# Low parts on VectorE, passes ordered by the weights' part, and a router with stationary weights

## The chip, the cores and the metric

The kernel runs on one core of a Trainium2 chip. The time is device microseconds of one execution; what counts is the median of several. The profile is that of one further execution on the same core.

## The reference

Two layers over 256 tokens of width 1024, with fp32 inputs and weights. Each layer is a token mixer (an mLSTM, a forgetting attention and an RWKV7 branch behind one wide projection), a cross attention to 256 memory tokens and a feed-forward part, each followed by a residual and a layer norm. The first layer's feed-forward part is dense; the second's is a mixture of eight experts of width 3584, of which each token takes two:

```python
def _post_norm(x, sub, g, b):
    return _layer_norm(DEEPNORM_ALPHA * x + sub, g, b)

def _swiglu(x, wgu, wd):
    gate, up = jnp.split(x @ wgu, 2, axis=-1)
    return (jax.nn.silu(gate) * up) @ wd

def _moe(x, router_w, router_b, ex_wgu, ex_wd):
    logits = (x @ router_w).astype(jnp.float32) + router_b
    top_v, top_i = lax.top_k(logits, TOP_K)
    top_w = jax.nn.softmax(top_v, axis=-1)
    comb = jnp.sum(jax.nn.one_hot(top_i, N_EXPERTS) * top_w[..., None], axis=-2)
    y = jnp.zeros_like(x)
    for e in range(N_EXPERTS):
        y = y + comb[..., e:e + 1] * _swiglu(x, ex_wgu[e], ex_wd[e])
    return y

for l in range(DEPTH):
    x = _post_norm(x, _token_mixer(x, ...), *ln1[l])
    x = _post_norm(x, _cross_attention(x, mem_n, *xattn[l]), *ln2[l])
    x = _post_norm(x, _swiglu(x, ...) if l % 2 == 0 else _moe(x, ...), *ln3[l])
```

## The kernel before

**Products in three passes.** Every operand of a large product is held as a high part, its fp32 value rounded to TensorE's fp32r type, and a low part, the difference. `mm3` (L323) adds three products in one PSUM tile: high weights with high x, high weights with low x, low weights with high x. It loops over the blocks `k` of 128 of the contraction and makes the three passes inside.

**Weights.** They pass through the core once, in chunks of 128 x 1024 fp32 (512 KB). `chunk` (L286) starts the load on SyncE's queue into a raw buffer (`raw`, L294), lets ScalarE cast it into the high part (`whi`, L295) and lets VectorE or GpSimd subtract for the low part (`wlo`, L297). GpSimd takes a low part when the list `self.aside` says so. `out_proj` (L389) fills that list, with `ASIDE = 3` entries that are true, at each of the five projections that end in a residual and a layer norm through it (the mixer's and the cross attention's in both layers, the dense part's in the first): 15 chunks of 912 in all. `out_proj` loads its last chunks, calls `mid()` and loads the norm's scale and shift before it issues its last products; this is so before and after.

**Buffers.** Rings of buffers are taken least recently used first: three raw buffers and three pairs of parts at the start, four more of each from the cross attention on, six more raw ones in the experts.

**Layer norm.** `residual` (L378) adds the projection's PSUM tile to x in two halves of 512 columns; `moments` (L351) takes statistics on VectorE and the power -0.5 on GpSimd (L364); `layer_norm` applies them on VectorE (L373, L374) half by half; `to_fm` (L339) transposes each half on TensorE and splits it into `xh` on ScalarE (L335) and `xl` on VectorE (L336). The two token halves are `tt`, the two column halves `h`.

**Experts' part.** `moe` (L1148) makes the logits of each token half with 16 products (L1195): a 128 x 128 block of x's high or low part is loaded as the stationary operand, and the router's 16 columns (high and low part of eight experts, `rwp`) move. VectorE adds bias and both parts (L1198, L1199), finds the two best (L1200, L1201), makes one-hot rows and counts (L1202 to L1211) with small products against triangular and all-one matrices (L1208 to L1213). ScalarE and GpSimd split x, tokens on partitions, into `xth` and `xtl` (L1220, L1221). `order` ranks the experts by their number of tokens. `experts` (L1283) gathers the tokens of a pair of experts by products with a 0/1 matrix `epb` (L1300, L1315); a pair has a large expert (128 slots, `mm3`) and a small one (64 slots). There are four pairs; `expert` runs over seven steps `c` of 512 hidden columns: `block` (L1343) the projections, `down` (L1365) the way back. In the small expert's `block` (L1355) the high and low parts of its x stand side by side as one stationary operand, and each block of weights moves twice, high and low part.

**Order.** The tile framework orders the instructions of each engine from a simulated timeline and from the order in which the program emits them, and puts in the semaphores; each engine then executes its list in order.

## Time and profile before

| | |
|---|---|
| median of 3 executions | 2165.76 us (2164.92 to 2166.17) |
| the profiled execution | 2165.97 us |
| its span, first to last instruction | 2164.2 us |
| mean granted clock of TensorE | 0.987 |
| TensorE, VectorE, ScalarE, GpSimd busy | 96%, 74%, 56%, 11% of the span |
| moved by the transfers | 532.18 MB, 246 GB/s on average |

A line of the profile gives busy time of an engine or of a group of instructions. Products on TensorE are pipelined, so the busy time of one is longer than the step from its start to the next. The rows below are in microseconds from the start of the span, if nothing else is said; a duration with xN is that of N such operations in a row.

### The profile page before, as it was taken

The page shows a single profiled execution, that of the slowest core. Times are in us where ns is not written, and L with a number is a line of the kernel's source. Part 1 is how long each engine was busy: PE and PEld are TensorE (multiplying, and loading weights), DVE is VectorE, ACT ScalarE, POOL GpSimd, SP SyncE. Part 2 cuts the span into 40 slices and gives each one's busy share as a digit, 9 for nine tenths or more (in the row PEclk, how much of TensorE's full clock was granted, in tenths as well). Part 3 has the DMA queues.
Part 4 walks back from the last instruction along what each step waited for, and adds up shares of the span by engine and source line. Part 5 has one row for each costly group of instructions (what it writes and reads, how often), then busy time and mean ns, then how long its engine had stood idle before and what let it go on. Part 6 is the DMA issues. An engine that isn't in the chain of part 4 may idle for free.

```text
span 2164.2 us, 33290 instructions
## 1 busy us (share of the span) xinstructions
PE 2082.1 (96%) x11726; PEld 1724.1 (80%) x11726; DVE 1601.9 (74%) x2327; ACT 1222.3 (56%) x1723; POOL 227.6 (11%) x332
## 2 busy tenths in 40 slices
PE   7999999999999899999998899999999999999996
PEld 6988898989998788889887777777767767777674
DVE  6776656746555677665675698889888988899887
ACT  5443334544443544332453587777777777777774
POOL 0031142202001113114212100000000000000000
PEclk9999999999999999999999799999999999999998
DMA  5431335645553543133574599999999999999994
GB/s 199 157 120 59 135 123 200 253 151 202 189 185 124 173 152 111 62 104 111 214 263 146 179 366 393 389 363 363 388 388 363 372 386 385 391 354 372 379 393 181
DMA packets 146767, 532.18 MB, mean 246 GB/s; under 512 B 16672, under 2 KB 17184, under 8 KB 145568
## 3 DMA queue, kind: packets, MB, share of 16 engines
q1 hardware_dynamic: 142128, 520.16, 64.9%
q10 hardware_dynamic: 4080, 8.77, 1.2%
q8 instruction: 94, 1.54, 0.3%
q0 software_dynamic: 384, 1.05, 0.1%
q14 instruction: 81, 0.66, 0.1%
HBM read 525.19 MB, written 4.72 MB: 245 GB/s over the span
## 4 chain that ended last, share of the span: by engine, by line
PE 52%; DMA 12%; DVE 10%; issue 3%; ACT 2%; POOL 1%; SPq 0%; DVEq 0%; ACTq 0%; POOLq 0%
DVE wlo L297 8%; DMA raw<-in_ex_wgu 7%; PE fps L331 7%; PE ops L331 6%; PE dps L331 6%; PE xps L331 5%; DMA raw<-in_ex_wd 5%; PE eacc L1372 4%; PE egu L331 4%; PE egu L1355 4%; PE eacc L331 2%; PE eacc L1379 2%; PE ups L331 2%; ACT whi L295 2%; PE eg L1315 1%
## 5 line engine op out<-in xcount | busy, mean ns | idle before, releaser
L297 DVE TENSOR_TENSOR wlo<-raw,whi 128x1024 fp32r<-128x1024 f32 x897 | 1073.9, 1231 | 261.4 <-ACT whi L295 251.5
L295 ACT CAST whi<-raw 128x1024 fp32r<-128x1024 f32 x912 | 916.2, 1049 | 468.0 <-PE fps L331 159.8
L331 PE MATMUL fps<-xh,whi 128*128 128x256 f32 x816 | 238.6, 293 | 7.5 <-ACT cu L543 4.9
L331 PE MATMUL fps<-xl,whi 128*128 128x256 f32 x816 | 235.0, 288 | 3.2 <-DVE xl L336 3.2
L331 PE MATMUL fps<-xh,wlo 128*128 128x256 f32 x816 | 236.4, 290 | 0.2
L1355 PE MATMUL egu<-wlo,xgs 128*128 128x512 f32 x448 | 198.1, 443 | 12.2 <-DVE wlo L297 12.2
L331 PE MATMUL egu<-wlo,xgh 128*128 128x512 f32 x448 | 178.9, 401 | 2.7 <-DVE wlo L297 2.6
L331 PE MATMUL egu<-whi,xgh 128*128 128x512 f32 x448 | 179.1, 401 | 0.8 <-ACT esl L1390 0.8
L331 PE MATMUL egu<-whi,xgl 128*128 128x512 f32 x448 | 178.2, 398 | 0.0
L1355 PE MATMUL egu<-whi,xgs 128*128 128x512 f32 x448 | 178.0, 398 | 0.0
L331 PEld LDWEIGHTS fps<-xh,whi 128*128 128x128 f32 x816 | 156.1, 191 | 13.9 <-ACT cu L543 5.7
L331 PEld LDWEIGHTS fps<-xl,whi 128*128 128x128 f32 x816 | 156.0, 191 | 5.7 <-DVE xl L336 3.5
L331 PEld LDWEIGHTS fps<-xh,wlo 128*128 128x128 f32 x816 | 156.0, 191 | 3.0 <-issue 2.0
L364 POOL TENSOR_TENSOR lnve<-lnve,mhalf 128x1 f32<-128x1 f32 x14 | 14.5, 1038 | 1282.2 <-DVE lnve L363 1282.2
L1355 PEld LDWEIGHTS egu<-wlo,xgs 128*128 128x128 f32 x448 | 84.0, 188 | 74.8 <-DVE wlo L297 60.9
L331 PE MATMUL eacc<-whi,ehl 128*128 128x512 f32 x448 | 124.6, 395 | 0.0
L331 PEld LDWEIGHTS egu<-wlo,xgh 128*128 128x128 f32 x448 | 84.7, 189 | 26.9 <-DVE wlo L297 7.8
L1372 PE MATMUL eacc<-raw,ehf 128*128 128x512 f32 x224 | 104.8, 594 | 0.1
L331 PEld LDWEIGHTS egu<-whi,xgl 128*128 128x128 f32 x448 | 84.8, 189 | 20.2 <-issue 0.7
L331 PEld LDWEIGHTS egu<-whi,xgh 128*128 128x128 f32 x448 | 84.5, 189 | 20.0 <-ACT esl L1390 1.0
L331 PEld LDWEIGHTS eacc<-whi,ehl 128*128 128x128 f32 x448 | 83.8, 188 | 20.0 <-DVE ehl L336 0.2
L331 PE MATMUL dps<-xl,whi 128*128 128x256 f32 x352 | 98.9, 281 | 0.6 <-DVE xl L336 0.6
(427 smaller groups left out, 4048.2 us busy)
## 6 DMA issues: line engine op xcount, KB each, us to landing
raw<-in_ex_wgu SPq DMA_DIRECT2D x448, 512.0 KB, 6.0
raw<-in_ex_wd SPq DMA_DIRECT2D x224, 512.0 KB, 5.8
raw<-in_w_fm SPq DMA_DIRECT2D x54, 512.0 KB, 3.3
raw<-in_w_gate SPq DMA_DIRECT2D x48, 512.0 KB, 3.2
raw<-in_ff_wgu SPq DMA_DIRECT2D x44, 512.0 KB, 4.3
raw<-in_w_tm SPq DMA_DIRECT2D x24, 512.0 KB, 3.3
raw<-in_ff_wd SPq DMA_DIRECT2D x22, 512.0 KB, 4.3
raw<-in_w_out SPq DMA_DIRECT2D x16, 512.0 KB, 3.9
```

Of the source, the lines that this page charges most:

```text
L295: nc.scalar.copy(hi[:, :e], raw[:, :e])
L297: eng.tensor_tensor(lo[:, :e], raw[:, :e], hi[:, :e].bitcast(F32), op=OP.subtract)
L331: nc.tensor.matmul(ps, l, r, start=first and n == 0, stop=last and n == 3 * kt - 1)
L364: nc.gpsimd.tensor_tensor(ve[:, 1:2], ve[:, 0:1], self.mhalf[:, 0:1], op=OP.pow)
L1315: nc.tensor.matmul(ps[:, kk, :n * P], src[:, tt, o], pb[:, tt, lo:hi].rearrange("p a b -> p (a b)"), start=tt == 0, stop=tt == 1)
L1355: nc.tensor.matmul(ps, x[2][:, 2 * q + kk], part[:, kk], start=q + kk + n == 0, stop=q == 3 and kk == 1 and n == 1)
L1372: nc.tensor.matmul(acc[h], ht[0][:, i], w[:, h * 512:(h + 1) * 512], start=f, stop=l)
L1379: nc.tensor.matmul(acc[h], ht[1][:, i - 2].rearrange("p a b -> p (a b)"), part[:, 0, s], start=f and n == 0, stop=l and n == 1)
```

## The change

Three edits.

1. All low parts go to VectorE: the list `aside` is gone, and the four subtractions for `xtl` move from GpSimd to VectorE, in a loop of their own behind ScalarE's four casts.
2. The pass is the outer loop in `mm3`: high weights with high x for every block `k`, then high weights with low x, then low weights with high x. In the small experts' `block`, both blocks take the high weights first, then both the low ones.
3. In the router the weights are stationary (128 x 16) and x moves (128 columns). The logits come out with the 16 columns on partitions; ScalarE copies them to SBUF, and a small product with a 16 x 8 matrix `fold`, made on GpSimd, brings the tokens back on partitions and adds high and low part. One addition of the bias is left. Conversion, one-hot rows, their sum and the positions are made for both token halves at once.

```diff
--- before.py
+++ after.py
@@ -58,7 +58,6 @@
 
 
 AHEAD = 2000
-ASIDE = 3
 FIRST = 65536.0
 RAWS = 6
 XGS = 5
@@ -293,8 +292,7 @@
         lo = pool.tile([P, 1024], F32R, name="wlo", tag="wlo", bufs=nparts)
         nc.sync.dma_start(raw[:, :e], src)
         nc.scalar.copy(hi[:, :e], raw[:, :e])
-        eng = nc.gpsimd if self.aside and self.aside.pop(0) else nc.vector
-        eng.tensor_tensor(lo[:, :e], raw[:, :e], hi[:, :e].bitcast(F32), op=OP.subtract)
+        nc.vector.tensor_tensor(lo[:, :e], raw[:, :e], hi[:, :e].bitcast(F32), op=OP.subtract)
         f = lambda t: t[:, :e].rearrange("p (k n) -> p k n", k=kt)
         return f(hi), f(lo)
 
@@ -324,8 +322,8 @@
 
         nc = self.nc
         n = 0
-        for k in range(kt):
-            for a, b in ((wh, xh), (wh, xl), (wl, xh)):
+        for a, b in ((wh, xh), (wh, xl), (wl, xh)):
+            for k in range(kt):
                 w, x = a[:, k, wsl], b[:, k, xsl]
                 l, r = (w, x) if w_stat else (x, w)
                 nc.tensor.matmul(ps, l, r, start=first and n == 0, stop=last and n == 3 * kt - 1)
@@ -402,7 +400,6 @@
         if mid:
             mid()
         gb = self.load_ln(lname)
-        self.aside = [False] * (7 - tail) + [True] * ASIDE
         for tt in range(2):
             for h in range(2):
                 for i, w in enumerate(ws):
@@ -1187,28 +1184,33 @@
             oh = wk.tile([P, 2, 2, NE], F32, name="eoh")
             sel = wk.tile([P, 2, NE], F32, name="esel")
             pos = wk.tile([P, 2, NE], F32, name="epos")
+            fold = wk.tile([2 * NE, NE], F32, name="efd")
+            nc.gpsimd.tensor_tensor(fold, self.ident[:2 * NE, :NE], self.ident[:2 * NE, NE:2 * NE], op=OP.add)
             pp = tp.tile([P, 5, NE], F32, name="epp", tag="t")
             for tt in range(2):
-                lp = self.gp.tile([P, 2, NE], F32, name="elp", tag="g")
+
+                lt = self.gp.tile([2 * NE, P], F32, name="elt", tag="g")
                 for k in range(KD):
                     for part in (xh, xl):
-                        nc.tensor.matmul(lp.rearrange("p a b -> p (a b)"), part[:, k, tt * P:(tt + 1) * P],
-                                         rwp[:, k].rearrange("p a b -> p (a b)"), start=k == 0 and part is xh,
-                                         stop=k == KD - 1 and part is xl)
-                nc.vector.tensor_tensor(lg[:, tt], lp[:, 0], rb, op=OP.add)
-                nc.vector.tensor_tensor(lg[:, tt], lg[:, tt], lp[:, 1], op=OP.add)
+                        nc.tensor.matmul(lt, rwp[:, k].rearrange("p a b -> p (a b)"), part[:, k, tt * P:(tt + 1) * P],
+                                         start=k == 0 and part is xh, stop=k == KD - 1 and part is xl)
+                ls = wk.tile([2 * NE, P], F32, name="els", bufs=2)
+                nc.scalar.copy(ls, lt)
+                nc.tensor.matmul(pp[:, 3 + tt], ls, fold, start=True, stop=True)
+                nc.vector.tensor_tensor(lg[:, tt], pp[:, 3 + tt], rb, op=OP.add)
                 nc.vector.max(mx[:, tt], lg[:, tt])
                 nc.vector.max_index(ix[:, tt], mx[:, tt], lg[:, tt])
-                nc.vector.tensor_copy(ixf[:, tt], ix[:, tt])
-                for k in range(2):
-                    nc.vector.tensor_scalar(oh[:, tt, k], it[:, :NE], ixf[:, tt, k:k + 1], None, op0=OP.is_equal)
-                nc.vector.tensor_tensor(sel[:, tt], oh[:, tt, 0], oh[:, tt, 1], op=OP.add)
+            nc.vector.tensor_copy(ixf, ix)
+            for k in range(2):
+                nc.vector.tensor_tensor(oh[:, :, k], it[:, None, :NE].to_broadcast([P, 2, NE]),
+                                        ixf[:, :, k:k + 1].to_broadcast([P, 2, NE]), op=OP.is_equal)
+            nc.vector.tensor_tensor(sel, oh[:, :, 0], oh[:, :, 1], op=OP.add)
             for tt in range(2):
                 if tt:
                     nc.tensor.matmul(pp[:, 1], ones, sel[:, 0], start=True, stop=False)
                 nc.tensor.matmul(pp[:, tt], self.c('strict'), sel[:, tt], start=tt == 0, stop=True)
-                nc.vector.scalar_tensor_tensor(pos[:, tt], pp[:, tt], 1.0, sel[:, tt], op0=OP.add, op1=OP.mult)
-                nc.vector.tensor_scalar(pos[:, tt], pos[:, tt], -1.0, None, op0=OP.add)
+            nc.vector.scalar_tensor_tensor(pos, pp[:, 0:2], 1.0, sel, op0=OP.add, op1=OP.mult)
+            nc.vector.tensor_scalar(pos, pos, -1.0, None, op0=OP.add)
             for tt in range(2):
                 nc.tensor.matmul(pp[:, 2], ones, sel[:, tt], start=tt == 0, stop=tt == 1)
 
@@ -1218,7 +1220,10 @@
                 for tt in range(2):
                     o = (slice(None), tt, slice(h * 512, (h + 1) * 512))
                     nc.scalar.copy(th[o], xt[o])
-                    nc.gpsimd.tensor_tensor(tl[o], xt[o], th[o].bitcast(F32), op=OP.subtract)
+            for h in range(2):
+                for tt in range(2):
+                    o = (slice(None), tt, slice(h * 512, (h + 1) * 512))
+                    nc.vector.tensor_tensor(tl[o], xt[o], th[o].bitcast(F32), op=OP.subtract)
 
             def order():
 
@@ -1350,8 +1355,8 @@
                         self.mm3(ps, wh, wl, x[0][:, k], x[1][:, k], 2, False, slice(0, 512), slice(0, P),
                                  first=q == 0, last=q == 3)
                         continue
-                    for kk in range(2):
-                        for n, part in enumerate((wh, wl)):
+                    for n, part in enumerate((wh, wl)):
+                        for kk in range(2):
                             nc.tensor.matmul(ps, x[2][:, 2 * q + kk], part[:, kk], start=q + kk + n == 0,
                                              stop=q == 3 and kk == 1 and n == 1)
                 if not small(j):
@@ -1473,7 +1478,7 @@
             for tt in range(2):
                 for h in range(2):
                     self.to_fm(self.tp, xt[:, tt], xh, xl, tt, h)
-        self.rings, self.aside, self.used, self.count = [], [], {}, 0
+        self.rings, self.used, self.count = [], {}, 0
         self.stream(self.ctx, 3, 3)
         stop = self.dbg.get('stop', 99)
         for l in range(2):
```

## Rows read from the trace of the kernel before

**Rows 1.** Busy time by stage: stretch, length, engines, TensorE's clock, transfers' share, GB/s.

```profile
0.00:1180.00 1180.00, 1144.24 (x7812) 1028.69 (x7812) 742.32 (x1406) 510.70 (x822) 213.21 (x317) 0.99 0.44 155
1180.00:1220.00 40.00, 27.59 (x121) 25.03 (x122) 28.47 (x73) 12.61 (x23) 12.46 (x14) 0.62 0.39 147
...
1317.00:2131.00 814.00, 796.36 (x3305) 584.10 (x3304) 723.92 (x733) 611.95 (x771) 0.00 (x0) 1.00 0.99 378
```

**Rows 2.** Groups of instructions: busy us, mean ns of one; idle time before.

```profile
L297 DVE TENSOR_TENSOR wlo<-raw,whi 128x1024 fp32r<-128x1024 f32 x897 | 1073.9, 1231 | 261.4 <-ACT whi L295 251.5
...
L297 POOL TENSOR_TENSOR wlo<-raw,whi 128x1024 fp32r<-128x1024 f32 x15 | 42.5, 2857 | 101.6 <-ACT whi L295 101.5
...
L336 DVE TENSOR_TENSOR xl<-tp,xh 128x512 fp32r<-128x512 f32 x24 | 15.8, 679 | 4.2 <-ACT xh L335 4.1
```

**Rows 3.** VectorE's timeline at two layer norms: start, us, operation, count.

```profile
385.31 1.40 DVE L373 SCALAR_TENSOR_TENSOR xt<-lnr,lnmv,lngb 128x512 f32<-128x512 f32 x2
...
390.28 2.83 DVE L297 TENSOR_TENSOR wlo<-raw,whi 128x1024 fp32r<-128x1024 f32 x1
...
500.06 4.74 DVE L373 SCALAR_TENSOR_TENSOR xt<-lnr,lnmv,lngb 128x512 f32<-128x512 f32 x2
```

**Rows 4.** The chain that ended last, by engine (page).

```profile
PE 52%; DMA 12%; DVE 10%; issue 3%; ACT 2%; POOL 1%; SPq 0%; DVEq 0%; ACTq 0%; POOLq 0%
```

**Rows 5.** TensorE's timeline at the start; in brackets the idle time before.

```profile
14.65 0.58 PE L331 MATMUL fps<-xl,whi 128*128 128x256 f32 x1 [3.23 <-DVE xl L336]
15.03 0.41 PE L331 MATMUL fps<-xh,wlo 128*128 128x256 f32 x1
...
18.87 0.32 PE L331 MATMUL fps<-xh,wlo 128*128 128x256 f32 x1
```

**Rows 6.** TensorE's timeline from the last norm to the first gather.

```profile
1186.47 1.94 PE L343 MATMUL tp<-ident,xt 128*128 128x128 f32 x8 [6.93 <-DVE xt L374]
...
1194.64 0.36 PE L1195 MATMUL elp<-rwp,xl 128*128 128x16 f32 x1
...
1197.62 0.36 PE L1195 MATMUL elp<-rwp,xl 128*128 128x16 f32 x1
...
1205.86 0.87 PE L1315 MATMUL eg<-epb,xth 128*128 128x128 f32 x3
```

**Rows 7.** GpSimd's timeline in the same stretch.

```profile
1179.83 2.35 POOL L297 TENSOR_TENSOR wlo<-raw,whi 128x1024 fp32r<-128x1024 f32 x1
...
1183.91 1.63 POOL L364 TENSOR_TENSOR lnve<-lnve,mhalf 128x1 f32<-128x1 f32 x1
...
1198.56 5.04 POOL L1221 TENSOR_TENSOR xtl<-xt,xth 128x512 fp32r<-128x512 f32 x4 [6.89 <-ACT xth L1220]
```

**Rows 8.** VectorE's timeline in the same stretch.

```profile
1180.84 2.55 DVE L373 SCALAR_TENSOR_TENSOR xt<-lnr,lnmv,lngb 128x512 f32<-128x512 f32 x2
...
1198.65 1.21 DVE L1211 TENSOR_SCALAR epos<-epos 128x8 f32<-128x8 f32 x1
...
1202.45 1.32 DVE L1204 TENSOR_SCALAR eoh<-eit,eixf 128x8 f32<-128x8 f32 x2
...
1205.08 0.17 DVE L1211 TENSOR_SCALAR epos<-epos 128x8 f32<-128x8 f32 x1
```

**Rows 9.** Groups of weight loads, of 64 and of 128 columns.

```profile
L331 PEld LDWEIGHTS fps<-xh,whi 128*128 128x128 f32 x816 | 156.1, 191 | 13.9 <-ACT cu L543 5.7
...
L746 PEld LDWEIGHTS fot<-fptb,fv 128*64 128x64 f32 x32 | 3.1, 134 | 2.1 <-issue 0.7
```

**Rows 10.** Waits: who waits, for whom: us, times, longest.

```profile
PEld egu L1355 <- DVE wlo L297: 60.9, 140, 1.1
...
PE egu L1355 <- DVE wlo L297: 12.2, 23, 0.8
```

**Rows 11.** Busy time by stage, ten microseconds each.

```profile
1200.00:1210.00 10.00, 6.16 (x25) 5.70 (x25) 8.22 (x33) 1.32 (x4) 3.60 (x3) 0.50 0.00 0
1210.00:1220.00 10.00, 10.00 (x46) 8.35 (x46) 4.88 (x4) 5.84 (x9) 0.00 (x0) 0.82 0.31 109
```

## Prediction

> **What bounds the kernel now.** I read the busy time by stage first [rows 1]. Up to 1180 us TensorE is the limit: busy 1144 of 1180 us, with VectorE at 742. From 1317 to 2131 us, the steady part of the experts, the transfers have a share of 0.99, TensorE is busy 796 of 814 and VectorE 724: three resources near their end at once. Between them lie 40 us, 1180 to 1220, in which no engine is full: TensorE 27.6 us, transfers 0.39. That is the last layer norm, the router, the counting of slots and the first gather, and it is the one stretch where a chain of short operations sets the time.
>
> The groups of instructions [rows 2] say what the edits can touch. VectorE makes 897 low parts at 1.231 us, GpSimd 15 at 2.857 us; these 15 sit in threes at five of the layer norms. The timeline of VectorE at two of those norms [rows 3] shows their side effect: two halves of a norm take 1.40 us when GpSimd is quiet, and 4.74 us at 500.06; a low part takes 2.83 us beside one of GpSimd's, not 1.23.
>
> The chain that ended last puts 52% on TensorE, 12% on transfers and 10% on VectorE [rows 4], so in the experts' loop nothing that saves one resource saves its full price.
>
> **Start of the kernel: -1.5 us (-2.9 to 0).** After one product with the high part of x TensorE waits 3.23 us, until 14.65, for x's low part [rows 5]. Products of 256 columns then start 0.213 us apart: 19 of them from 15.03 to 18.87, 3.84 / 18, which is TensorE's lower clock level, 1.2 GHz. With the passes outermost, the seven other high products of the first chunk stand ahead of the first that needs the low part: 7 x 0.213 = 1.5 us of work fits into the wait. At most the wait itself goes, less some 0.3 us for handing over: 2.9. Nothing, if the other high parts of x aren't there in time.
>
> **Twelve low parts at the first four norms: -0.4 us (-1 to +1).** VectorE gets 12 x 1.231 = 14.8 us. It gets back the blocking: I estimate four low parts stretched by 1.6 us as at 390.28 (6.4), and 2 us of stretched norm at each of four norms, between the 0 of 385.31 and the 3.3 of 500.06 (8.0) [rows 3]: 14.4 us. So its load there is unchanged. What hides the rest is TensorE, which has products of other chunks to do and is busy 97% of this stage [rows 1]; the norm of each half comes a little earlier. If that cover were gone, all 14.8 us would be bare; that is the last rival.
>
> **The last norm: -1.4 us (-2.6 to +1.1).** Here there is no cover: TensorE waits 6.93 us for the normalised x, until 1186.47 [rows 6]. The wait is made by GpSimd: its low part of 1179.83 takes 2.35 us, copies follow, and the power for the standard deviation starts at 1183.91 [rows 7], though VectorE had its input done before the norm's first two halves at 1180.84; these took 2.55 us, not 1.40 [rows 8]. Without the low part ahead of it, the power can come some 2.6 us earlier. But that low part, 1.23 us, is now queued on VectorE near by: 2.6 - 1.2 = 1.4. All three of this norm in front of it would make 3.7 - 2.6 = +1.1.
>
> **Router with narrow weights: -1.5 us (-2.7 to +0.7).** Now x is loaded (128 columns) and 16 columns move; the rows from 1194.64 to 1197.62 are 15 products, so one each 2.98 / 14 = 0.213 us, 32 in all [rows 6]. After the change 16 columns are loaded and 128 move. No row has such a shape. It can't be worse than 0.213: the gather's products from 1205.86 load 128 columns and move 128 at that step (0.87 us for three with the drain of the last). Below, half of a 256-column product at this clock gives 0.107 [rows 5]. I take 0.12, nearer to the moving columns, since 64-column loads are shorter too, 134 ns against 191 ns for 128 columns [rows 9]. Of 32 x 0.093 = 3.0 us, the products between two waits for x's parts give nothing back. The 15 from 1194.64 on stand behind the last low part and count in full; of the 17 others I count 8, those that hold up transposes of the other token half: 23 x 0.093 = 2.1. Against it stand a copy of 128 columns on ScalarE (0.25, an estimate between the 0.17 of VectorE's smallest operations [rows 8] and the 0.68 of its 512 columns [rows 2]), a small product that folds high and low (0.6, an estimate: a step of 0.213 and the handovers on both sides), less one addition on VectorE (0.2): +0.65. Together -1.5; the ends are -3.4 + 0.65 and 0 + 0.65.
>
> The Trainium skill, "TensorE: Matmul & The Clock Gate", section LDWEIGHTS (loading the stationary operand), has the load go by columns, one per 1/1.2 ns: 16 columns 13 ns against 107 for 128. The rows agree that fewer columns load faster, not on the size [rows 9]. By that page the load would vanish behind the moving columns, 23 products at 0.107: 2.4 us saved instead of 2.1.
>
> **Counting and gather: -2.7 us (-4.1 to -1.3).** From 1198.56 GpSimd makes the four low parts for the gather, 5.04 us [rows 7]. In the same time five small operations on VectorE, on 2 to 8 columns, take 4.91 us, from the 1.21 at 1198.65 to the two in 1.32 at 1202.45; the first one's line takes 0.17 at 1205.08, after GpSimd is done [rows 8]. At 0.17 each they are 0.85: 4.06 us of blocking on the path from the logits to the first gather at 1205.86. It goes; in its place VectorE itself makes the four low parts, at 0.679 each as x's low parts of the same shape [rows 2], 2.7 us. They stand behind ScalarE's casts and can slip into the gaps in which VectorE waits for the small products; I let half of them fall on the path: -4.06 + 1.35. Merged operations for both token halves save another few tenths, and the first half's positions now wait for the second's; I set these against each other.
>
> **Pass order in the experts: -3.3 us (-6.7 to 0).** In the small experts' projections TensorE's loads wait for a low part 140 times, 60.9 us, and its products 23 times, 12.2 us [rows 10]. With both high parts first, one 512-column product moves ahead of each wait, 0.24 us (796 / 3305 [rows 1]). But the next chunk is as late as before, so per step of the loop I count one product, at most: 28 steps (four pairs of experts, seven each) x 0.24 = 6.7 us. If the transfers pace the loop, at a share of 0.99, it is 0. Half is taken, as the chain gives TensorE the larger part of it [rows 4].
>
> **Sum.** -1.5 - 0.4 - 1.4 - 1.5 - 2.7 - 3.3 = -10.8 us against the profiled execution's 2165.97 (span 2164.2 and 1.8 outside it), which is within 0.01% of the median 2165.76. That gives **2155.2 us**.
>
> **Rivals.**
> *The edges close again (0.20).* The router's edits get nothing: the low parts moved to VectorE stand ahead of the norm (0 for the last norm), the narrow products are no faster than their fold costs (0), half the counting's gain is lost (-1.3), and the loop is paced by transfers, so that pass order does nothing there (0). With -1.5 and -0.4 for the first stage: 2165.97 - 3.2 = 2162.8. For it speaks the 0.99 [rows 1]; against it that VectorE's stretched operations are plainly on the path [rows 8].
> *The clock comes back sooner (0.20).* TensorE runs at 0.50 of its clock from 1200 to 1210 and at 0.82 on average from 1210 to 1220 [rows 11], so the lower level, 1.2 GHz, lasts for 3.6 us of the latter, to 1213.6. Before it rose, TensorE had been busy 6.2 of 10 us and then without a break. The products from 1205.86 [rows 6] to 1213.6 are 7.7 us at that level; if the shorter chain leaves fewer holes and the clock is up by then, half goes, 3.9. With the loop's full 6.7: -10.8 - 3.9 - 3.4 = -18.1, 2147.9.
> *VectorE becomes the limit (0.10, the other side).* 15 x 1.231 + 4 x 0.679 = 21.2 us more on VectorE; if it lands on the path at the norms while the relief falls where nobody waits, and the start (1.5), the narrow router (1.5) and the loop (3.3) still give theirs: +21.2 - 6.3 = +14.9, 2180.9. It decides from 10.6 of the 21.2 bare (6.3 + 4.3). Against it: 742 busy of 1180 [rows 1], and the stretched rows. The Trainium skill, "Perfetto Trace Analysis", section Optimizing Scalar/DVE Operations, speaks for it: with a saturated VectorE, moving work to GpSimd may make sense, which this undoes; the same paragraph doubts it, as the two share a port. The stretched rows are that doubt, measured [rows 3].
>
> **How the numbers follow.** The sum has 0.50, with a range of its own of 2150 to 2160. The range, 2147 to 2163, takes in the two faster-side rivals and leaves out the slower one. A measurement of this kernel tells some 0.2%, 4.3 us, from no change. Faster by more: 0.50 + 0.20 and a quarter of the first rival, 0.75; within it 0.15; slower 0.10.
>
> **What would show it.** No low part on GpSimd, and none of VectorE's at 2.8 us; the halves of all norms at 0.7. TensorE's first wait for x's low part at 1.7 us, not 3.2. The wait before the last transposes at 5.5 us. Router products 0.12 us apart, the small operations of counting at 0.17, the first gather 5 to 6 us sooner; the stretch between the last norm and 1317 shorter by about 6 us, and the steady loop by 3. Wrong would be the prediction if VectorE's low parts push the norms later, if the loop's length moves by more than 7 us either way, since nothing here prices that, or if the order of work elsewhere changes with the new costs.

## The result, and the profile after

The changed kernel takes 2155.01 us (median of 5, 2149.88 to 2155.67) against 2166.17 of before: a ratio of 0.9941, 95% interval 0.9925 to 0.9957. Measured a second time it was 0.9943 (0.9929 to 0.9956). The forecast was 2155.2, in a range of 2147 to 2163. The profiled execution took 2149.88 us, span 2147.7: 16.5 us less span than before's 2164.2. It is the fastest of its five; the median execution is 5.1 us slower. Where the 16.5 us went, stage by stage, is a matter of the trace; that the sum came out is not yet a proof of its terms.

Busy time by stage of the changed kernel, against [rows 1]:

```profile
0.00:1180.00 1180.00, 1144.98 (x7812) 1030.47 (x7812) 742.39 (x1419) 517.55 (x822) 182.58 (x308) 0.99 0.45 155
1180.00:1220.00 40.00, 28.78 (x154) 25.30 (x154) 28.07 (x74) 16.76 (x31) 2.96 (x4) 0.74 0.47 168
...
1317.00:2131.00 814.00, 799.33 (x3336) 591.06 (x3336) 729.32 (x741) 614.74 (x777) 0.00 (x0) 1.00 0.97 376
```

The first 1180 us are as full as they were, 1145 us of TensorE. In the 40 us behind them GpSimd has gone from 12.5 to 3.0 us, the transfers have more, and TensorE's clock is at 0.74, not 0.62. Groups and waits of the changed kernel, against [rows 2, 10]:

```profile
L295 DVE TENSOR_TENSOR wlo<-raw,whi 128x1024 fp32r<-128x1024 f32 x912 | 1088.9, 1230 | 229.3 <-ACT whi L294 196.2
```

```profile
PEld egu L1360 <- DVE wlo L295: 51.9, 113, 1.0
...
PE egu L1360 <- DVE wlo L295: 12.0, 23, 0.5
```

All 912 low parts are VectorE's, at 1.230 us on average. The waits of the small experts' loads are 51.9 us, 113 times; they were 60.9, 140 times.

TensorE's and VectorE's timelines from the last norm to the first gather, against [rows 6, 8], and GpSimd's, against [rows 7]:

```profile
1186.04 1.94 PE L341 MATMUL tp<-ident,xt 128*128 128x128 f32 x8 [6.78 <-DVE xt L372]
...
1191.98 0.31 PE L1195 MATMUL elt<-xh,rwp 128*16 128x128 f32 x1
...
1193.05 0.31 PE L1195 MATMUL elt<-xh,rwp 128*16 128x128 f32 x1
...
1194.29 0.22 PE L1195 MATMUL elt<-xl,rwp 128*16 128x128 f32 x1
1195.32 0.38 PE L1199 MATMUL epp<-efd,els 16*128 16x8 f32 x2 [0.81 <-ACT els L1198]
...
1201.23 1.09 PE L1320 MATMUL eg<-epb,xth 128*128 128x128 f32 x4
```

```profile
1180.63 1.21 DVE L295 TENSOR_TENSOR wlo<-raw,whi 128x1024 fp32r<-128x1024 f32 x1
1181.75 0.20 DVE L359 BATCH_NORM_AGGREGATE lnmv<-lnst 128x2 f32<-128x12 f32 x1
1181.87 1.17 DVE L295 TENSOR_TENSOR wlo<-raw,whi 128x1024 fp32r<-128x1024 f32 x1
...
1183.69 0.15 DVE L361 TENSOR_SCALAR lnve<-lnmv 128x1 f32<-128x1 f32 x1
1183.75 1.41 DVE L371 SCALAR_TENSOR_TENSOR xt<-lnr,lnmv,lngb 128x512 f32<-128x512 f32 x2
...
1195.75 0.16 DVE L1200 TENSOR_TENSOR elg<-epp,rb 128x8 f32<-128x8 f32 x1
1195.83 0.69 DVE L1226 TENSOR_TENSOR xtl<-xt,xth 128x512 fp32r<-128x512 f32 x1
...
1196.51 0.68 DVE L1226 TENSOR_TENSOR xtl<-xt,xth 128x512 fp32r<-128x512 f32 x1
...
1197.30 0.69 DVE L1226 TENSOR_TENSOR xtl<-xt,xth 128x512 fp32r<-128x512 f32 x1
...
1198.11 0.26 DVE L1205 TENSOR_TENSOR eoh<-eit,eixf 128x16 f32<-128x16 f32 x2
...
1200.34 0.17 DVE L1213 TENSOR_SCALAR epos<-epos 128x16 f32<-128x16 f32 x1
```

```profile
1183.92 0.99 POOL L362 TENSOR_TENSOR lnve<-lnve,mhalf 128x1 f32<-128x1 f32 x1 [24.58 <-DVE lnve L361]
```

In before, the first bias addition of the second token half, which ends the router there, is this row:

```profile
1198.02 0.17 DVE L1198 TENSOR_TENSOR elg<-elp,rb 128x8 f32<-128x8 f32 x1 [1.77 <-PE elp L1195]
```

Cut at the same places, the two profiles give this. "The gather" is its run of products, from 1205.86 and from 1201.23; in before a single product of it stands ahead of that run, at 1201.41.

| stretch | before | after | difference |
|---|---|---|---|
| start to TensorE's stop at the last norm (1186.47 - 6.93; 1186.04 - 6.78) | 1179.54 | 1179.26 | -0.3 |
| wait for the norm | 6.93 | 6.78 | -0.15 |
| transposes and router, to the last router product | 11.15 | 8.25 | -2.9 |
| from there to the gather | 8.24 | 6.94 | -1.3 |
| from there to the end of the span | 958.3 | 946.5 | -11.9 |

The norm gave nothing, router and counting together 4.2 us, which is what the two terms said (1.5 + 2.7). The copy and the fold belong to the router's term: cut behind them, at the bias addition (1198.02 before, 1195.75 after), the router gave 1.8 us and the counting 2.4. The experts gave three to four times their term.

Why the norm gave nothing is in VectorE's rows. The power now starts on GpSimd without a stretched neighbour, but at 1183.92; it was 1183.91. On VectorE one low part, 1180.63, stands ahead of the norm's aggregate, and another, 1181.87, between the aggregate and the small operation at 1183.69 from which GpSimd takes its input; the first halves start at 1183.75 in place of 1180.84. What GpSimd held up, VectorE's own queue now holds up.

In the router x's products are 0.107 us apart (11 from 1191.98 to 1193.05, 1.07 / 10). The copy and the fold between the last one and the first addition of the second half take 1.46 us (1194.29 to 1195.75). From there the small operations take 0.17 us each, and the two one-hot rows 0.26. But three of the four low parts of x for the gather stand among them (1195.83, 1196.51, 1197.30), 0.6 us each from its start to the next: 1.8 us on the path, where the prediction let half of the four, 1.35, fall on it.

TensorE's clock after, against [rows 11]:

```profile
1190.00:1200.00 10.00, 6.26 (x47) 5.72 (x45) 6.48 (x27) 3.96 (x9) 0.95 (x2) 0.67 0.30 119
1200.00:1210.00 10.00, 9.73 (x41) 8.67 (x41) 5.37 (x23) 3.75 (x7) 0.00 (x0) 0.65 0.00 1
1210.00:1220.00 10.00, 10.00 (x57) 8.49 (x55) 6.22 (x6) 7.24 (x11) 0.00 (x0) 1.00 0.77 246
```

It is up again for part of the router (0.67), falls once more, and is at its upper level throughout 1210 to 1220. With 0.65 from 1200 to 1210 the lower level ends at 1207.0 (10 x 0.35 / 0.5), 5.8 us after the gather's start; before it was 7.7 us after it.

The start, against [rows 5], and TensorE's waits in the first 62 us (total, times, longest):

```profile
10.74 2.07 PE L329 MATMUL fps<-xh,whi 128*128 128x256 f32 x8 [0.35 <-ACT xh L333]
12.62 2.05 PE L329 MATMUL fps<-xl,whi 128*128 128x256 f32 x8
14.46 1.72 PE L329 MATMUL fps<-xh,wlo 128*128 128x256 f32 x8
```

```profile
PE tp L638 <- DVE grow L635: 2.0, 1, 2.0
PE rza L759 <- ACT lw L762: 1.2, 1, 1.2
...
PE fps L329 <- DVE mv L554: 0.4, 1, 0.4
```

Eight high products run, and the low part of x is there when they end: the wait of 3.23 us is gone. Two waits of 2.0 and 1.2 us further on are new. Only a part of this is the order of passes. Ahead of x's low part VectorE makes two small casts, and these differ between the two profiles, first before, then after:

```profile
11.48 2.52 DVE L270 CAST keep<-cst 128x128 uint8<-128x128 f32 x2
```

```profile
11.38 0.56 DVE L269 CAST keep<-cst 128x128 uint8<-128x128 f32 x2
```

Beside them GpSimd fills a buffer in eight operations, in both kernels. In before the casts end at 14.00 with the last of these (13.86); in the changed kernel they pass between them, and two of the eight take 0.66 us in place of 0.52. Which of the two happens is a matter of the single execution: of the 14 traces of this document, seven have the casts long and seven short, and the three traces that share the changed kernel's first part have both.

### The profile page after: what moved, and what is told of

Read it like the earlier page. It is cut to its first block, busy times and chain, and to the rows that moved or that the text cites. A ratio compares the mean times of both kernels' runs of the same rounds, so it can differ in the third digit from the quotient of the medians.

```text
span 2147.7 us, 33270 instructions
## 1 busy us (share of the span) xinstructions
PE 2071.4 (96%) x11730; PEld 1723.0 (80%) x11730; DVE 1598.2 (74%) x2338; ACT 1227.1 (57%) x1725; POOL 187.4 (9%) x314
## 4 chain that ended last, share of the span: by engine, by line
PE 67%; DMA 11%; DVE 10%; issue 4%; ACT 4%; POOL 3%; SPq 0%; POOLq 0%; DVEq 0%; ACTq 0%
PE fps L329 14%; DVE wlo L295 7%; PE ops L329 7%; DMA raw<-in_ex_wgu 6%; PE xps L329 6%; PE egu L329 6%; PE dps L329 6%; DMA raw<-in_ex_wd 4%; PE egu L1360 4%; PE eacc L1377 4%; PE ups L329 3%; ACT whi L294 3%; PE eacc L329 2%; PE rg L857 2%; PE eacc L1384 1%
## 5 line engine op out<-in xcount | busy, mean ns | idle before, releaser
L329 PE MATMUL egu<-whi,xgh 128*128 128x512 f32 x448 | 142.3, 399 | 0.8 <-ACT esl L1395 0.8
L1360 PE MATMUL egu<-whi,xgs 128*128 128x512 f32 x448 | 141.1, 397 | 0.7 <-ACT whi L294 0.7
L329 PE MATMUL egu<-wlo,xgh 128*128 128x512 f32 x448 | 140.8, 398 | 0.0
L329 PE MATMUL fps<-xh,whi 128*128 128x256 f32 x816 | 127.9, 295 | 2.6 <-ACT xh L333 1.7
L1360 PEld LDWEIGHTS egu<-wlo,xgs 128*128 128x128 f32 x448 | 75.1, 188 | 67.4 <-DVE wlo L295 51.9
L329 PE MATMUL fps<-xl,whi 128*128 128x256 f32 x816 | 127.5, 291 | 0.0
L329 PE MATMUL fps<-xh,wlo 128*128 128x256 f32 x816 | 124.4, 288 | 0.0
L329 PEld LDWEIGHTS fps<-xh,whi 128*128 128x128 f32 x816 | 109.0, 194 | 9.8 <-issue 3.5
L329 PEld LDWEIGHTS fps<-xl,whi 128*128 128x128 f32 x816 | 110.1, 193 | 2.3 <-issue 1.7
L329 PEld LDWEIGHTS fps<-xh,wlo 128*128 128x128 f32 x816 | 107.9, 190 | 2.8 <-issue 2.5
L1360 PEld LDWEIGHTS egu<-whi,xgs 128*128 128x128 f32 x448 | 83.5, 188 | 21.2 <-ACT whi L294 2.2
```

The costliest lines, as they stand in the source:

```text
L329: nc.tensor.matmul(ps, l, r, start=first and n == 0, stop=last and n == 3 * kt - 1)
L1360: nc.tensor.matmul(ps, x[2][:, 2 * q + kk], part[:, kk], start=q + kk + n == 0, stop=q == 3 and kk == 1 and n == 1)
```

## The experiments

Each was timed in five rounds beside the kernel before. Lengths come from each run's trace: the end of the last projection (its last product's start), the head (from there to the first product of an expert) and the loop (from there to the last product of a way back). The tail is 18.4 to 18.6 us in all but one. "Slow clock" is the time at TensorE's lower level ahead of the last projection's end; the last column takes half of it off. That is what it costs where TensorE is the limit: in the second layer, from the mixer's output projection to the cross attention's, TensorE takes 59.8 us in before, without such a stretch, and 61.1 to 61.5 in the five other traces with the same instructions and one stretch of 3.4 us there.

| run | ratio to before (95%) | head | loop | last projection's end | slow clock | less its half |
|---|---|---|---|---|---|---|
| before | | 29.1 | 937.5 | 1179.1 | 13.7 | 1172.3 |
| the change | 0.9941 (0.9925 to 0.9957) | 25.0 | 925.4 | 1178.9 | 17.1 | 1170.3 |
| changed_again | 0.9943 (0.9929 to 0.9956) | 25.7 | 925.0 | 1179.3 | 20.5 | 1169.1 |
| passes_alone | 0.9968 (0.9958 to 0.9978) | 29.1 | 924.8 | 1183.0 | 13.7 | 1176.2 |
| small_block_alone | 0.9986 (0.9977 to 0.9995) | 29.1 | 933.0 | 1182.8 | 20.5 | 1172.5 |
| mm3_alone | 1.0005 (0.9995 to 1.0015) | 29.1 | 930.9 | 1188.0 | 23.9 | 1176.1 |
| lows_alone | 1.0028 (1.0018 to 1.0037) | 29.0 | 937.8 | 1182.1 | 17.1 | 1173.6 |
| xlow_alone | 0.9989 (0.9980 to 0.9998) | 27.2 | 935.6 | 1176.0 | 10.2 | 1170.8 |
| router_alone | 0.9993 (0.9984 to 1.0001) | 26.0 | 937.0 | 1181.9 | 20.5 | 1171.7 |
| gpsimd_lows_back | 0.9955 (0.9942 to 0.9968) | 25.4 | 925.2 | 1185.4 | 13.7 | 1178.6 |
| experts_only | 0.9925 (0.9912 to 0.9937) | 25.6 | 925.4 | 1183.3 | 20.5 | 1173.0 |
| low_pass_behind | 0.9915 (0.9901 to 0.9930) | 26.5 | 916.7 | 1184.6 | 23.9 | 1172.6 |
| experts_only_behind | 0.9891 (0.9875 to 0.9906) | 25.5 | 916.3 | 1180.8 | 20.5 | 1170.5 |
| two_chunks_behind | 0.9898 (0.9881 to 0.9914) | 25.2 | 920.3 | 1180.8 | 17.1 | 1172.3 |

Where the instructions are the same, loops repeat within 0.4 us (925.0 to 925.4 in four runs) and heads within 0.7 (25.0 to 25.7 in the same four). The first part doesn't: before, xlow_alone, router_alone, small_block_alone and the three runs named experts_only, experts_only_behind and two_chunks_behind have the same instructions up to the last projection's end, and come to it between 1176.0 and 1183.3. With the slow clock taken off it is 1170.5 to 1173.0. low_pass_behind has the changed kernel's instructions up to there, so that one is at 1169.1 to 1172.6 in its three traces. Part of what is left is the start: of its first 12.9 to 20.8 us the traces have no record of the granted clock (a row shows 1.00 for it), though products of 256 columns stand 0.213 us apart there and 0.118 behind it, and the two casts are long or short. (That TensorE is at 1.2 GHz there, as the prediction has it, is read from this pace.) Two windows of before and of xlow_alone show slow stretches in different places; TensorE's clock is the third number from the end:

```profile
1060.00:1080.00 20.00, 17.59 (x80) 14.36 (x79) 16.48 (x19) 11.76 (x15) 6.71 (x6) 0.83 0.90 348
1125.00:1145.00 20.00, 17.94 (x123) 16.45 (x122) 8.67 (x16) 9.20 (x20) 0.00 (x0) 1.00 0.30 106
```

```profile
1060.00:1080.00 20.00, 17.59 (x83) 14.19 (x83) 16.46 (x19) 11.36 (x16) 4.63 (x4) 1.00 0.94 367
1125.00:1145.00 20.00, 17.93 (x111) 15.74 (x109) 7.65 (x16) 8.24 (x18) 0.00 (x0) 0.91 0.22 74
```

In one execution the slow stretch is at 1060 to 1080 (0.83), in the other at 1125 to 1145 (0.91). So a few microseconds of one profile's first part say nothing on a change; head and loop do.

### Each edit alone

**passes_alone**

```diff
-        for k in range(kt):
-            for a, b in ((wh, xh), (wh, xl), (wl, xh)):
+        for a, b in ((wh, xh), (wh, xl), (wl, xh)):
+            for k in range(kt):
...
-                    for kk in range(2):
-                        for n, part in enumerate((wh, wl)):
+                    for n, part in enumerate((wh, wl)):
+                        for kk in range(2):
```

> The kernel before with the order of passes alone (the pass outermost in mm3 and the high weights first in the small experts' block); low parts and router as before. Theory A, the prediction's terms: 1.5 us at the start and 3.3 us in the experts' loop, 4.8 us faster than before, about 2161. Theory B, after the trace of the changed kernel, in which the loop from the first expert's product to the end is some 10 to 12 us shorter and the first 1179 us are not: the loop's gain is this edit's alone, 8 to 12 us faster, 2154 to 2158, with the last layer norm's end where it was within 1 us. Theory C: the loop's pace is set by the transfers and the shift comes from the head: within 2 us of before.

0.9968: 6.9 us. The loop is 12.7 us shorter, so theory B has the loop right, but not the total (8 to 12): the first part got 3.9 us longer, slow clock taken off, and gives a third of it back. VectorE's and TensorE's timelines of this run at the second layer's first norm show one place:

```profile
1093.45 2.30 DVE L374 SCALAR_TENSOR_TENSOR xt<-xt,lnve,lngb 128x512 f32<-128x512 f32 x1
...
1096.27 2.29 DVE L374 SCALAR_TENSOR_TENSOR xt<-xt,lnve,lngb 128x512 f32<-128x512 f32 x1
...
1100.23 2.83 DVE L297 TENSOR_TENSOR wlo<-raw,whi 128x1024 fp32r<-128x1024 f32 x1
```

```profile
1103.77 0.39 PE L331 MATMUL xps<-wlo,mem 128*128 128x512 f32 x1
1107.18 0.63 PE L343 MATMUL tp<-ident,xt 128*128 128x128 f32 x4 [3.02 <-issue]
```

GpSimd's three low parts stretch two halves of the norm to 2.3 us and a low part to 2.83. TensorE has run out of other products and stands for 3.0 us until the second halves, behind all this, are normalised. That norm was covered in before; with the new order of the work ahead of it, it isn't.

**lows_alone**

```diff
...
-        eng = nc.gpsimd if self.aside and self.aside.pop(0) else nc.vector
-        eng.tensor_tensor(lo[:, :e], raw[:, :e], hi[:, :e].bitcast(F32), op=OP.subtract)
+        nc.vector.tensor_tensor(lo[:, :e], raw[:, :e], hi[:, :e].bitcast(F32), op=OP.subtract)
...
```

> The kernel before with the fifteen low parts of the weights moved from GpSimd to VectorE, and nothing else; the router's low parts of x stay on GpSimd. Theory A, the prediction's terms: 0.4 us at the first four norms and 1.4 us at the last, 1.8 us faster, about 2164. Theory B: the low parts now stand ahead of the norms on VectorE, as at 1180.63 and 1181.87 in the changed kernel, so that the norms end no sooner or up to 4 us later: 0 to 4 us slower.

1.0028: 6.1 us slower. Theory A, the prediction's, falls, and theory B has the sign; its bound was 4 us. TensorE's timeline at the norm ahead of the dense part shows what theory B said, two waits of 1.55 and 1.17 us for the norm's halves:

```profile
509.89 0.63 PE L341 MATMUL tp<-ident,xt 128*128 128x128 f32 x4 [1.55 <-DVE xt L372]
511.69 0.63 PE L341 MATMUL tp<-ident,xt 128*128 128x128 f32 x4 [1.17 <-DVE xt L372]
512.07 0.36 PE L329 MATMUL dps<-xh,whi 128*128 128x256 f32 x1
```

In before the dense part's first product started 0.1 us after the last product of the work ahead. The head is 0.15 us shorter: the last norm gives next to nothing. Of the 6.1 us the profile, slow clock taken off, accounts for 1.2 (1173.6 against 1172.3). Most of the rest goes with the clock: the mean granted clock of the nine executions is 0.9850, that of the 33 of before beside them 0.9873. Over the run that is 32.6 and 27.6 us lost to the lower level, 5.0 of the 6.0 by which the mean times differ. That the new waits are what lets the clock fall more often fits, but isn't shown.

**xlow_alone**

```diff
-                    nc.gpsimd.tensor_tensor(tl[o], xt[o], th[o].bitcast(F32), op=OP.subtract)
+            for h in range(2):
+                for tt in range(2):
+                    o = (slice(None), tt, slice(h * 512, (h + 1) * 512))
+                    nc.vector.tensor_tensor(tl[o], xt[o], th[o].bitcast(F32), op=OP.subtract)
```

> The kernel before with the four low parts of x for the gather (xtl) moved from GpSimd to VectorE, and nothing else. Theory A, the prediction's term: the small operations of counting take 0.17 us again, 2.7 us faster, and this delta passes through the loop to the end. Theory B: VectorE makes the four at once ahead of the chain, 0 to 1 us faster. Theory C: the first expert's product comes sooner but the loop takes it back, as transfers or buffers set its pace: under 1 us faster at the end.

0.9989, 2.4 us: the size of theory A's 2.7, though the interval (0.4 to 4.3) takes in theories B and C as well. The head is 1.9 us shorter and the loop 1.9; the framework gave the loop another order than in before, so that the second 1.9 is not the edit's own.

**router_alone** is the router's part of the change's diff, nothing else.

> The kernel before with the router's edit alone (stationary weights, the fold, merged small operations); low parts and passes as before. Theory A, the prediction's term with what the changed kernel's trace shows of it: products 0.107 us apart, 1.5 to 2.5 us off the head of the experts. Theory B: with GpSimd's low parts still running beside it, the chain is blocked at the same place and the gain is under 1 us, or the fold's extra steps make it up to 1 us slower.

0.9993 (0.9984 to 1.0001), 1.5 us, not clear of nothing by itself. The head is 3.1 us shorter, more than theory A. With the low parts of x it doesn't add up: 3.1 and 1.9 alone, 3.5 together in experts_only.

### Which order of passes it is

**small_block_alone** is the second part of the diff of passes_alone.

> The kernel before with the order of passes changed in the small experts' block alone (both high parts of the weights before both low ones); mm3 as before. In the run with both orders changed, the stretch from the first expert's product to the last was 12.7 us shorter than before, 0.45 us for each of the 28 steps of the loop. Theory A: this edit is the one that meets the waits for low parts in the rows of before, and gives nearly all, 10 to 13 us in that stretch and 8 to 12 at the end. Theory B: it gives one product a step, up to 6.7 us, and mm3 the rest. Theory C: mm3 gives nearly all and this edit under 2 us.

**mm3_alone** is the first part.

> The kernel before with the pass outermost in mm3 alone; the small experts' block as before. Theory A: nothing in the experts' stretch (within 2 us), as the large experts' products seldom wait for a low part, and in the first 1180 us the order of other work changes and costs 2 to 6 us: as before or up to 6 us slower. Theory B: 5 to 7 us less in the experts' stretch. Theory C: 10 to 13 us less there.

The loop is 4.5 us shorter with small_block_alone and 6.6 with mm3_alone; 11.1 in sum, 12.7 together. For both runs theory B holds. Per step (28) that is 0.16 and 0.24 us, which is two thirds of the time of one 512-column product and all of it, though in mm3 two products move ahead of the first that needs a low part, and in the small block one. mm3 pays for its 6.6 us ahead of the experts, 3.8 us with the slow clock taken off, and comes out at 1.0005; the mean granted clock of its twelve executions is lower too, 0.9857 against 0.9871, which is 3 us.

### The move of the low parts inside the changed kernel

**gpsimd_lows_back** is the changed kernel with the lines of lows_alone turned back.

> The changed kernel with the fifteen low parts of the weights back on GpSimd; everything else stays changed, the low parts of x on VectorE too. Theory A: the move costs here what it cost alone, some 6 us, all of it ahead of the experts: 2148 to 2150. Theory B: with the passes outermost a low part is needed one to seven products later, so the move costs nothing in the changed kernel: 2154 to 2156, the last norm aside. Theory C: the prediction's term, the move gains 1.8 us: 2156 to 2158.

0.9955 against 0.9941 and 0.9943: some 3 us slower with GpSimd than without, in intervals that overlap. Theory A falls; C has the side. Its first part is 1178.6 with the slow clock off, the changed kernel's 1170.3, 1169.1 and, in low_pass_behind, 1172.6. The last has the long casts at the start, as this run has, so that like against like the difference is 6.0 us. From the last product of the mixer's output projection to the first of the cross attention's, in the second layer, it takes 67.1 us, with one slow stretch of 3.4; the changed kernel 62.5, with none.

**changed_again** is the changed kernel itself.

> The changed kernel once more, beside the two that follow. In the profiles so far the head of the experts and the loop repeat to 0.1 us wherever the instructions are the same, while the first 1180 us differ by up to 7 us between executions of the same instructions, with the number of stretches at TensorE's lower clock. Theory A: the second profile of the changed kernel has 25.0 us from the last projection to the first expert's product and 925.4 us of loop again, and all that differs lies ahead of them: the cross attentions' share stays at 82 and 62 us, if the move of the low parts is what made them short, and the number of slow-clock stretches differs. Theory B: the cross attentions take 85 and 66 us or more, as in the other kernels with the passes outermost; then the first profile of the changed kernel was a lucky one and moving the low parts did nothing there.

Theory A: the loop is 925.0, and between the two output projections of a layer lie 81.7 and 64.1 us (81.7 and 62.5 in the first profile), the second with one slow stretch of 3.4 us in it; with the passes outermost and GpSimd's low parts it was 85.3 and 65.8 in passes_alone. The low parts' move is what makes them short again: before had 83.3 and 59.8. The head is 0.7 us longer than in the first profile, which theory A did not have.

### Versions

**experts_only** takes the kernel before, passes a flag to mm3 in the experts alone, and has the small block's order, the low parts of x and the router of the change. The weights' low parts stay as in before.

```diff
-        for k in range(kt):
-            for a, b in ((wh, xh), (wh, xl), (wl, xh)):
+        parts, ks = ((wh, xh), (wh, xl), (wl, xh)), range(kt)
+        for a, b, k in ([(a, b, k) for a, b in parts for k in ks] if outer else
+                        [(a, b, k) for k in ks for a, b in parts]):
...
-                                 first=q == 0, last=q == 3)
+                                 first=q == 0, last=q == 3, outer=True)
```

> The kernel before with only those edits that gave something in the stretch where they stand: the order of passes in the experts alone (large and small; mm3 elsewhere with the passes inside), the low parts of x on VectorE, and the router; the fifteen low parts of the weights stay on GpSimd. The first 1179 us then have the instructions of before. Theory A: the edits outside the experts cost 3 to 6 us and are now gone: 12 us from the loop and 4 to 5 from the head give 2148 to 2150, faster than the changed kernel by 5 to 7. Theory B: the first stage's difference is the scatter of single executions, so this equals the changed kernel within 2 us.

0.9925 (0.9912 to 0.9937), 16 us, all of it from head and loop; by the ratios that is 3 to 4 us below the changed kernel, in intervals that overlap. Between A and B the runs don't decide.

**low_pass_behind** delays, on the changed kernel, the low pass in the experts' projections by one chunk. `passes` issues the products of one chunk `q`, for each pair of weights' part and x's part that it is given:

```diff
...
+                xs = (x[2],) if small(j) else (x[0], x[1])
+                late = None
                 for q in range(4):
                     wh, wl = self.chunk(wgu(i * GE + c, q), 2, 512)
...
+                    passes(q, [(wh, xx) for xx in xs], q == 0, False)
+                    if late:
+                        passes(q - 1, late, False, False)
+                    late = [(wl, xs[0])]
+                passes(3, late, False, True)
```

> The changed kernel with the low pass of each chunk in the experts' projections one chunk later: the high passes of chunk q + 1 stand ahead of the low pass of chunk q, in large and small experts. Theory A: TensorE's waits for low parts pace the loop; each high product that stands ahead of such a wait gave up to 0.24 us a step so far, so two to four more give 6 to 15 us: 2140 to 2149. Theory B: what was left of those waits is hidden by the transfers, whose share is 0.97 to 1.00 in the changed kernel: within 2 us of it. Theory C: buffers of high and low parts are held longer, loads start later: slower by up to 5 us.

The loop falls to 916.7, by 8.3 to 8.7 us: theory A. By the ratios the total falls by 6 us; the head is 0.9 to 1.6 us longer and the tail 2.0. Its waits, and one window of the loop in before, in the changed kernel and in this one (TensorE busy first, transfers' share and GB/s last):

```profile
PEld egu L1355 <- DVE wlo L295: 20.0, 42, 1.0
```

```profile
1317.00:2100.00 783.00, 766.99 (x3190) 564.11 (x3190) 695.41 (x702) 587.88 (x743) 0.00 (x0) 1.00 0.99 378
```

```profile
1317.00:2100.00 783.00, 770.38 (x3224) 571.67 (x3224) 704.06 (x711) 596.15 (x753) 0.00 (x0) 1.00 0.99 383
```

```profile
1317.00:2100.00 783.00, 773.78 (x3262) 579.23 (x3261) 710.86 (x719) 601.23 (x759) 0.00 (x0) 1.00 1.00 386
```

The same 783 us hold 3190, 3224 and 3262 products, at 378, 383 and 386 GB/s. A share of 0.99 was no wall: with the waits for low parts shorter, the transfers moved 2% more.

**experts_only_behind** is the same edit on experts_only.

> The kernel with the passes reordered in the experts alone and the weights' low parts of the first stage on GpSimd, with the low pass one chunk later in the experts. The same three theories for the loop, on the other first stage: its loop equals that of the run before within 0.5 us, and its total lies below that run's by 0 to 4 us.

2142.81 us, 0.9891 (0.9875 to 0.9906): 23.6 us faster than before and the fastest that was run. The loop is 916.3, equal to the run before's 916.7 as expected; the total lies 5 to 6 us below that run's, not 0 to 4.

**two_chunks_behind** delays the low pass by two.

> As experts_only_behind, with the low pass two chunks later in the experts' projections, not one. One chunk took 8.7 to 9.0 us off the loop (925.4 to 916.5) and left 20.0 us of waits for low parts, 42 times, of 51.9, 113 times. Theory A: waits still pace the loop; the rest of them goes and the loop is 3 to 6 us shorter, 910 to 913. Theory B: the transfers, share 1.00 at 386 GB/s in that loop, now pace it: 915 to 917. Theory C: parts are held longer and the seven pairs of buffers run out: 918 or more.

The loop is 920.3, 4 us longer than with one. Its waits:

```profile
PEld egu L1359 <- ACT whi L295: 34.4, 65, 1.6
...
PE egu L1359 <- ACT whi L295: 16.1, 22, 1.2
...
PEld egu L1359 <- DVE wlo L297: 10.1, 22, 0.5
```

Those for low parts halve again, to 10.1 us, but TensorE now waits for ScalarE's high parts, 34.4 and 16.1 us. Theory C has the sign; that the pairs of buffers run out, its reason, isn't shown.

## Why the prediction was right, and where it was not

The forecast time held: 2155.2 against 2155.0, and 2151.7 the second time. Its mechanism held in part only, and that the two numbers meet is luck. In the profile the change gave 16.5 us, not 10.8: the experts gave 8.6 more than their term, the first part and the last norm 2.9 less. The median execution then is 5.1 us slower than the profiled one. By its own last paragraph the prediction would be wrong if the loop's length moved by more than 7 us, if VectorE's low parts pushed the norms later, or if the order of work elsewhere changed: the loop moved by 12, TensorE waits 2.20 us for the norm ahead of the dense part where it waited 0.40, and the new order of passes uncovered the norms.

**Start: the wait fell by what the term said, but the gain wasn't kept.** TensorE was idle for 11.7 of the first 62 us before (62 - 20.13 - 30.18 by the windows 0 to 30 and 30 to 62) and for 10.1 after: 1.6 us, where the term had 1.5. But before's profile has the two casts long, and the changed kernel's has them short. Where they are long, the wait for x's low part is 3.2 to 3.5 us with the old order (five traces) and 2.0 with the new (two); where they are short, 1.4 (three) and 0 (four). So the order takes 1.2 to 1.5 us off it. Further on a wait of 1.8 us for ScalarE goes, and in all six traces of the new order waits of 2.0 and 0.4 us come, which take most of the gain back: like against like TensorE's idle time in the 62 us is 11.5 to 11.9 and 11.2 to 11.3 with long casts, 9.7 to 9.8 and 9.1 to 10.1 with short ones.

**First four norms: the step failed, though the sum hid it.** It said that the load is unchanged and TensorE's other products hide the rest. Cover isn't a property of the stage but of the order of work at each norm. With the old order of passes the move costs (lows_alone, 1.0028); with the new one the norms are uncovered, GpSimd's stretching shows on TensorE (1107.18 in passes_alone), and the same move helps. Move and pass order are one edit here: slow clock taken off, the first part is 3.9 us longer with the order alone and 1.2 longer with the move alone. With both it is 1169.1 to 1172.6 in three traces, where the instructions of before are at 1170.5 to 1173.0 in seven: what the move gains is what the order had lost, and no gain over before stands clear of the scatter. Pass order outside the experts had no term at all beyond the start. The waits show in the changed kernel too; VectorE's and TensorE's rows at the norm ahead of the dense part, against [rows 3]:

```profile
497.76 2.34 DVE L295 TENSOR_TENSOR wlo<-raw,whi 128x1024 fp32r<-128x1024 f32 x2
...
500.62 2.35 DVE L295 TENSOR_TENSOR wlo<-raw,whi 128x1024 fp32r<-128x1024 f32 x2
...
508.56 1.40 DVE L371 SCALAR_TENSOR_TENSOR xt<-lnr,lnmv,lngb 128x512 f32<-128x512 f32 x2
```

```profile
512.26 1.29 PE L341 MATMUL tp<-ident,xt 128*128 128x128 f32 x8 [2.20 <-DVE xt L372]
```

No operation is stretched, the halves are at 0.70 us, but low parts stand between the norm's steps and TensorE waits 2.20 us.

**Last norm: the step failed.** It let one low part of 1.2 us fall on the path against 2.6 us won. Two stand ahead of the operation that gives GpSimd its input, and 0.15 us is left. It was within its bounds (+1.1).

**Router and counting: right.** They gave -1.8 and -2.4 us, where the terms had -1.5 and -2.7; in the other runs with both edits the head is 2.6 to 3.9 us shorter than before's. The split hangs on what stands beside them, since alone the two gave 3.1 and 1.9. Products came 0.107 us apart at the lower clock level, the lower bound, where 0.12 was taken; the last seven were at 0.06, behind a return of the clock at 1193.4 that no term had. By the Trainium skill, "TensorE: Matmul & The Clock Gate", section LDWEIGHTS (loading the stationary operand), a load goes by its columns; that the narrow load vanishes behind the 128 moving columns agrees with this 0.107.

**Pass order in the experts: mechanism right, size wrong.** The term had 28 x 0.24 = 6.7 as its most and half as its value; head aside, the stretch gave 11.9, beyond the bound. The step that failed is "per step of the loop I count one product": it looked at the small experts' block alone, where the larger wait stands, and there the 4.5 us of small_block_alone lie within it. mm3 in the large experts, which had no term, gives another 6.6 us. The trace of before had a row for it that was not used, loads of large experts' products waiting 7.8 us for a low part, 20 times; in the changed kernel that row is gone.

**The rivals.** "The edges close again" had the last norm right, at 0, and the rest not. That the transfers pace the loop fell: at shares of 0.99 to 1.00 it went from 937.5 to 925.4 and 916.7 us. That the clock comes back sooner came true in part: its lower level after the gather's start is 5.8 us long, not 7.7, worth about 1 us where 3.9 was said. That VectorE becomes the limit did not happen to the whole, but is what lows_alone shows on a small scale: GpSimd's help, undone, cost 6.1 us there, most of it by way of the clock. The Trainium skill's "Perfetto Trace Analysis", section Optimizing Scalar/DVE Operations, has both halves: such an offload may make sense, and the shared port may spoil it; here the order of TensorE's work decided which.

**What stays open.** Head and loop are 16 us shorter in both profiles of the changed kernel, and the medians 11 to 14. Two things on record go that way. Both profiles have the short casts, and long ones cost 2.0 us more of wait. And the granted clock of the profiles is 0.9884 and 0.9875 (49.7 and 53.5 us at the lower level), the mean of the ten executions 0.9872, which is 1 to 3 us; before's mean is 0.9873, so that the change as a whole doesn't run at a lower clock. How often the casts are long in executions without a trace isn't known, nor why the move alone goes with a lower clock.

## What to carry to other kernels

A wait for a late operand is best met by putting work that doesn't need it ahead of the wait, in the order of the queue; count every place where the same helper stands before such a wait, not the one with the largest row, and try the delay by one chunk more. Moving work between two engines that disturb each other and changing what covers them can't be priced apart: run both edits alone and together. A transfer share of 0.99 is not a floor as long as the rate still rises when buffers come free earlier. Where executions of one kernel differ by more than an edit is worth, as the first part does here, compare several traces that had the same luck, not one with one.

## What the runs showed of the hardware

Executions of the same instructions repeat a stage of TensorE's work to some 0.02 us (the dense part's products, first to last, 125.16 to 125.20 us in seven profiles). What differs between executions are stretches of 3.4 or 6.8 us at TensorE's lower clock level, three to six ahead of the last norm and not always in the same places, each worth half its length where TensorE is the limit (59.8 us for a stage without, 61.1 to 61.5 with one of 3.4).

VectorE's operations of 128 x 512 elements went from 0.75 to 2.3 us and more, and small ones of eight columns from 0.17 to 1.2, beside GpSimd's subtractions; with GpSimd quiet every one of them is at its short time. Beside GpSimd's eight fills of 0.52 us at the start two small casts of VectorE either end just behind the last fill and take 2.5 to 2.8 us together, or they pass in 0.6 to 0.7 us and two of the fills take 0.66: seven traces each, with the same instructions on both sides.
